# A hybrid decoder layer in fp32 on one core: low weight parts of the first attention on VectorE, and its background steps spread anew

## The chip, the core and the metric

The kernel runs on one core of a Trainium2 chip. The metric is the time of one execution on the device in microseconds (us), from the first to the last instruction and what lies around them. Three runs of the kernel before took 1514.23, 1518.8 and 1519.63 us; the median is 1518.8 us. The engines are named as in the profile: PE is TensorE (matmuls, with PEld its weight loads), DVE is VectorE, ACT is ScalarE, POOL is GpSimd, and SP issues the DMAs.

## What is computed

One layer on 1024 tokens of width 2048: an RMS norm with a shift and a scale that come from a conditioning vector c, one input projection into eight parts, a gated branch (spatial mixing in chunks of 128), an attention branch (window of 128, 16 query heads, 4 key heads, a learned sink), one output projection, a gate, and a last norm with a second shift and scale.

```python
shift, scale, gate = split(silu(c) @ w_ada + b_ada, 3)
h = rms_norm(x, norm_g) * (1 + scale) + shift
u, v, z_a, q, k, v_b, z_b = split(h @ w_in)
y_a = u * (tril(W_s) @ layer_norm(v) + b)
y_b = window_attention_with_sink(rope(q), rope(k), v_b)
x = x + gate * (concat(y_a * silu(z_a), y_b * silu(z_b)) @ w_out)
out = rms_norm(x, final_norm_g) * (1 + scale_f) + shift_f
```

## The kernel before

The tokens are worked in two halves of 512. Every fp32 product is made of three matmuls (`mm3`, L205 to L208): both operands are split into a high part, rounded to the matmul's own format, and a low part, the rest. For the weights this is done as they come in: `chunk` (L127) fetches 128 x 1024 values by DMA, and `split_w` (L138) makes of each 128 x 512 tile a high part with ACT (L148) and a low part, "lo" below, by one subtraction (L149). There are three buffers for each part. The engine of the subtraction is POOL where `on_pool` holds, else DVE.

The input projection is cut into groups of 512 columns (u0, u1, kv, q0, q1, va0, va1, zb0, zb1, za0, za1). `project` (L265) makes one group for one half of the tokens: 16 steps ("kt") of 12 matmuls, a split for each, a DMA for every second. `half(h, kq)` (L766) runs half h: q1, va1, zb0, zb1, u0, u1, za0, za1, then the output projection. Attention is a generator (`attention`, L394, 32 units and 3 steps of tail): from the seventh step of q1 on, `tick` (L242) advances it at 0.58 units per kt, so that its small matmuls stand between those of q1, va1, zb0 and zb1. Its softmax is a chain over PE, DVE and ACT: scores (L335, L336), their least value (DVE L339, L341), exponentials (ACT L343, L344), sums and division (DVE L345 to L348), transposes (PE L355), a split (ACT L359, DVE L360), values (PE L367, L368), and the sum into y (DVE L375, L376). The rotary embedding (`rope`, L287) uses DVE and POOL in turn, also in the background of q1, va1 and zb0. u0 carries the spatial mixing.

Beside that runs the background `bg`: generators whose steps `project` calls after every second kt (`bgn`, L279 and L280). In the first half it holds, in this order, `corr_bg` (8 steps: a row of the shift is loaded into the one tile `misc` by L202, two pieces of the va weights by L736, and four products with sums by DVE L742; at its end a transpose by PE, L195), `gate_bg` (32 steps: one piece of the adaLN weights by L160 and one product with a sum by DVE, L165, a "gate multiply" below) and `stat_bg` (8 steps). A scheduler sets each engine's final order from the program order and priorities; the engines then run their rows strictly in that order.

In the first half alone (`h == 0`) the lo of the weights from q1 to u0 are made by POOL (L788, L821).

```python
lo_pool[0] = h == 0
q1 = project(["q1"], ["mm"], bgn=(0, 1) if h else (1,), after_kt=start)["q1"]
ps = project(["va1"], ["mm"], bgn=(0, 1) if h else (1,))["va1"]
silu_gate(project(["zb0"], ["mm"], bgn=(0, 1) if h else (1, 1, 1, 1, 1, 1, 2, 1))["zb0"], 4, 16)
zb1 = project(["zb1"], ["mm"], bgn=(h,), after_kt=ln_step)["zb1"]
```

Of the kernel before, what the change touches and what calls it, by code (L numbers as in the profile page):

```python
# [31 lines left out]
def R(t):  # L32
    return t.bitcast(F32R)
# [3 lines left out]
def hybrid_layer(ctx: ExitStack, tc: tile.TileContext, A, out):  # L37
# [22 lines left out]
    def four(tag):  # L60
        return banks8[tag]
# [56 lines left out]
    def flat(t):  # L118
        return t.rearrange("p a b -> p (a b)")

    lo_pool = [False]
    ahead = [False]

    def boost():
        return tc.high_priority() if ahead[0] else nullcontext()

    def chunk(src):  # L127
        r = turn_of(raws)
        nw[0] += 1
        with boost():  # L130
            if nw[0] < 3:
                for i in range(2):
                    sp.dma_start(out=r[:, i, :], in_=src[:, i, :])
            else:
                sp.dma_start(out=r, in_=src)
        return r

    def split_w(r, kk, keep=None, on_pool=False):  # L138
        i = nw[1] % 3
        nw[1] += 1  # L140
        with boost():
            if keep is not None:
                act.activation(R(keep[:, :256]), r[:, kk, 256:], AF.Copy)
                dve.tensor_tensor(R(keep[:, 256:512]), r[:, kk, 256:], keep[:, :256], op=ALU.subtract)
                act.activation(R(w_hi[i][:, :256]), r[:, kk, :256], AF.Copy)
                dve.tensor_tensor(R(w_lo[i][:, :256]), r[:, kk, :256], w_hi[i][:, :256], op=ALU.subtract)
                return R(w_hi[i]), R(w_lo[i])
            act.activation(R(w_hi[i]), r[:, kk, :], AF.Copy)  # L148
            (pool if on_pool else dve).tensor_tensor(R(w_lo[i]), r[:, kk, :], w_hi[i], op=ALU.subtract)  # L149
        return R(w_hi[i]), R(w_lo[i])  # L150
# [54 lines left out]
    def mm3(o, lh, ll, rh, rl, first, last):  # L205
        pe.matmul(o, lhsT=lh, rhs=rh, start=first, stop=False)  # L206
        pe.matmul(o, lhsT=lh, rhs=rl, start=False, stop=False)  # L207
        pe.matmul(o, lhsT=ll, rhs=rh, start=False, stop=last)  # L208

    Hh, Hl = [None] * KT, [None] * KT  # L210

    def feature_major(ps, c, W, kt):
        w = slice(c * P, c * P + P)
        mm3(ps, W[0][:, w], W[1][:, w], R(Hh[kt]), R(Hl[kt]), kt == 0, kt == KT - 1)

    def token_major(ps, t, W, kt, w, opens=True, closes=True):
        tk = slice(t * P, t * P + P)
        mm3(ps, R(Hh[kt])[:, tk], R(Hl[kt])[:, tk], W[0][:, w], W[1][:, w], opens and kt == 0, closes and kt == KT - 1)

    def kt_step(g, banks, W, kt):  # L220
        if g == "kv":
            for c in range(2):
                feature_major(banks[c], c, W, kt)
            for t in range(4):
                token_major(banks[2 + t // 2][:, (t % 2) * 256:(t % 2) * 256 + 256], t, W, kt, slice(256, 512),
                            t % 2 == 0, t % 2 == 1)
        elif g in ("va0", "va1"):
            for t in range(4):
                token_major(banks[t], t, W, kt, slice(0, 512))
        else:  # L230
            for c in range(4):
                feature_major(banks[c], c, W, kt)
# [9 lines left out]
    def tick():  # L242
        credit[0] += credit[1]
        while credit[0] >= 1 and side:
            credit[0] -= 1
            try:
                next(side[0])
                settle()
            except StopIteration:
                side.pop(0)  # L250
# [6 lines left out]
    def background(n):  # L257
        while n > 0 and bg:
            try:
                next(bg[0])  # L260
                n -= 1
            except StopIteration:
                bg.popleft()

    def project(gs, tags, per_kt=None, bgn=None, after_kt=None, pool_lo=(), steps=None):  # L265
        banks = {g: four(t) for g, t in zip(gs, tags)}
        raw = {}
        for kt, g in steps or [(kt, g) for kt in range(KT) for g in gs]:
            if g == gs[0] and per_kt is not None:
                per_kt(kt)  # L270
            if (g, kt // 2) not in raw:
                raw[g, kt // 2] = chunk(A["win"][GI[g], kt // 2])
            W = split_w(raw[g, kt // 2], kt % 2, on_pool=lo_pool[0] or (g in pool_lo and kt > 1))
            kt_step(g, banks[g], W, kt)
            if g == gs[-1]:
                if after_kt is not None:
                    after_kt(kt)
                tick()
                if bgn and kt % 2:  # L279
                    background(bgn[kt // 2 % len(bgn)])  # L280
        return banks

    def grab(dst, ps):
        with tc.high_priority():
            act.activation(dst, ps, AF.Copy)
# [14 lines left out]
    def k_stack(parts, j):  # L300
        h1, h2, l1, l2 = parts
        rs = slice(32 * j, 32 * j + 32)
        for k, (a, b) in ((K1[j], (h1, h2)), (K2[j], (l1, l2))):
            for r, s in enumerate((a, b, a, b)):
                sp.dma_start(out=k[32 * r:32 * r + 32, P:], in_=s[rs])
# [72 lines left out]
    def x_pair(kv):  # L378
        return Y[4 + kv][:, 0, :], Y[4 + kv][:, 1, :]
# [6 lines left out]
    def rope_q(kv):  # L386
        parts[kv] = rope(*x_pair(kv), *tpair(kv), *cs)

    def stack(kv, pair):
        Qs[kv, pair] = q_stack(parts[kv], pair)  # L390
# [87 lines left out]
    def settle():  # L478
        while waiting and done[0] >= waiting[0][1]:
            z_mul(waiting.pop(0)[0])  # L480

    def silu_gate(ps, base, need=0):
        for c in range(4):
            with tc.high_priority():
                act.activation(zz[c], ps[c], AF.Silu)  # L485
        waiting.append((base, need))
        settle()
# [197 lines left out]
    for kt in range(KT):  # L685
        g1_kt(kt)
        if kt % 2 == 0:
            raw = chunk(A["win"][GI["va0"], kt // 2])
        W = split_w(raw, kt % 2, on_pool=kt > 1)
# [76 lines left out]
    def half(h, kq):  # L766
        ahead[0] = True
        done[0], credit[0], credit[1] = 0, 0.0, 0.0
        for i, n in enumerate(("cos", "sin")):
            sp.dma_start(out=cs[i], in_=A[n][h])  # L770
        for i in range(2):
            grab(zz[2 + i], kq["kv"][i])

        def q_grab(ps, kvs):
            for i in range(4):
                grab(x_pair(kvs[i // 2])[i % 2], ps[i])

        q_grab(kq["q0"], (0, 1))
        kparts = rope(zz[2], zz[3], zz[0], zz[1], *cs)
        k_stack(kparts, 0)  # L780
        rope_q(0)
        stack(0, 0)
        v_stage(kq["kv"][2:])
        stack(0, 1)
        for j in range(1, 4):
            k_stack(kparts, j)

        lo_pool[0] = h == 0  # L788
        side.append(attention(h))

        def start(kt):
            if kt == 6:
                credit[0], credit[1] = 0.0, 0.58

        q1 = project(["q1"], ["mm"], bgn=(0, 1) if h else (1,), after_kt=start)["q1"]
        q_grab(q1, (2, 3))
        ps = project(["va1"], ["mm"], bgn=(0, 1) if h else (1,))["va1"]
        for t in range(4):
            grab(Y[t][:, 1, :], ps[t])
            if h:  # L800
                sp.dma_start(out=Y[t][:, 0, :], in_=v_d[t])
        silu_gate(project(["zb0"], ["mm"], bgn=(0, 1) if h else (1, 1, 1, 1, 1, 1, 2, 1))["zb0"], 4, 16)
        ln = norm_v(h)

        def ln_step(kt):
            if kt >= 4:
                next(ln, None)

        zb1 = project(["zb1"], ["mm"], bgn=(h,), after_kt=ln_step)["zb1"]
        for _ in ln:  # L810
            pass
        silu_gate(zb1, 6, 32)
        held = [rings.popleft(), rings.popleft()]
        wr = prep_spatial(h, held)
        side.append(spatial(*wr))
        ps = project(["u0"], ["mm"], bgn=(h,))["u0"]
        drain()
        rings.extend(held)
        if h == 0:
            join()  # L820
        lo_pool[0] = False  # L821
        u_gate(ps, 0, S_[:4])
        u_gate(project(["u1"], ["mm"], bgn=(1,))["u1"], 2, S_[4:])
        silu_gate(project(["za0"], ["mm"], bgn=(1,))["za0"], 0)

        def release(kt):
            frr(Hh[kt], Hl[kt])

        ps = project(["za1"], ["mm"], bgn=(1,), after_kt=release)["za1"]
        split_y((4, 5, 6, 7))  # L830
        split_y((0, 1))
        silu_gate(ps, 2)
        split_y((2, 3))
        if h:
            background(1000)
            fr(*[cb[:, 512 * i:512 * i + 512] for i in range(4)])
        out_phase(h)
# [94 lines left out]
```

## Time and profile before

| | before |
|---|---|
| median of three runs | 1518.8 us |
| the profiled execution: its time, its span | 1516.88 us, 1515.1 us |
| busy in the span: PE, DVE, ACT, POOL | 1447.4, 960.8, 629.8, 256.2 us |
| TensorE's granted clock, mean | 0.99 |
| q1 to u0 of the first half: length, DVE busy, POOL busy | 308.3, 200.3, 136.0 us |
| q1 to u0 of the second half: length, DVE busy, POOL busy | 278.7, 216.6, 28.1 us |

Busy time is time in which the engine works on at least one instruction; matmuls are pipelined and their ends are modelled, so a busy PE is not PE at its peak. A stretch here begins with the first matmul of one group and ends with the first matmul of the next. In an engine's row a releaser (<-) is what ended its idle time. Line numbers are those of the kernel before.

### The profile page before, as it was taken

Reading aid. Unit: us, or ns where it says so; the run is one execution under the profiler, and the core shown is the slowest. Engines: PE = TensorE matmul, PEld = TensorE weight load, DVE = VectorE, ACT = ScalarE, POOL = GpSimd, SP = SyncE. Lnnn points to the kernel's source line nnn. Section 1 sums busy time; section 2 is a strip of 40 time slices with the busy share of each in tenths; the row PEclk is TensorE's granted clock in tenths of the full one; section 3 lists DMA queues with packets and bytes.
Section 4 is the critical chain, followed back from the end, with each engine's and each line's share of the span. In section 5 each row is a group of like instructions: output and inputs, shape, how many; then the busy total and the mean of one; then the engine's idle time right before and its main releaser. Section 6 shows DMA issues by size and latency. Waiting matters only on the chain. (4 is left out here: it accounts for less than half of the span.)

```text
span 1515.1 us, 20294 instructions
## 1 busy us (share of the span) xinstructions
PE 1447.4 (96%) x7049; PEld 1208.2 (80%) x7049; DVE 960.8 (63%) x1905; ACT 629.8 (42%) x1397; POOL 256.2 (17%) x184
## 2 busy tenths in 40 slices
PE   7998999888899999999999999999999999999997
PEld 5777877767688888888888978878888878888897
DVE  6879774688763353333466556888796555556456
ACT  3443335454664223432334323666764222332341
POOL 1322164433535100110000101000101001010002
PEclk9999999999999999999999999999999999999999
DMA  9978765556523366733555756544445666665422
GB/s 360 343 294 287 275 190 144 182 172 222 174 70 119 125 198 195 262 120 104 172 159 190 242 184 180 180 126 138 147 154 173 198 211 207 210 229 194 140 84 111
DMA packets 90409, 282.74 MB, mean 187 GB/s; under 512 B 12273, under 2 KB 12865, under 8 KB 90306
## 3 DMA queue, kind: packets, MB, share of 16 engines
q1 hardware_dynamic: 90162, 280.92, 57.0%
q8 instruction: 55, 0.90, 0.2%
q10 hardware_dynamic: 144, 0.52, 0.1%
q14 instruction: 48, 0.39, 0.1%
HBM read 254.10 MB, written 14.72 MB: 177 GB/s over the span
## 5 line engine op out<-in xcount | busy, mean ns | idle before, releaser
L208 PE MATMUL mm<-r,wl 128*128 128x512 f32 x1024 | 401.1, 392 | 9.0 <-DVE wl L149 4.8
L206 PE MATMUL mm<-r,wh 128*128 128x512 f32 x1024 | 402.2, 393 | 5.0 <-ACT wh L148 2.5
L207 PE MATMUL mm<-r,wh 128*128 128x512 f32 x1024 | 400.6, 391 | 0.0
L148 ACT ACTIVATE wh<-wr 128x512 fp32r<-128x512 f32 x324 | 201.7, 627 | 355.7 <-PE mm L207 195.2
L208 PEld LDWEIGHTS mm<-r,wl 128*128 128x128 f32 x1024 | 192.9, 188 | 55.1 <-DVE wl L149 8.7
L149 DVE TENSOR_TENSOR wl<-wr,wh 128x512 fp32r<-128x512 f32 x220 | 154.8, 708 | 127.6 <-ACT wh L148 117.2
L206 PEld LDWEIGHTS mm<-r,wh 128*128 128x128 f32 x1024 | 193.1, 189 | 44.8 <-ACT wh L148 3.4
L207 PEld LDWEIGHTS mm<-r,wh 128*128 128x128 f32 x1024 | 193.2, 189 | 37.4
L149 POOL TENSOR_TENSOR wl<-wr,wh 128x512 fp32r<-128x512 f32 x104 | 151.3, 1459 | 293.8 <-ACT wh L148 271.6
L206 PE MATMUL mm<-wh,r 128*128 128x512 f32 (+1 forms) x448 | 169.1, 381 | 8.0 <-ACT wh L148 8.0
L207 PE MATMUL mm<-wl,r 128*128 128x512 f32 (+1 forms) x448 | 171.3, 382 | 4.9 <-POOL wl L149 4.9
L208 PE MATMUL mm<-wh,r 128*128 128x512 f32 (+1 forms) x448 | 169.9, 380 | 0.0
L207 PE MATMUL att<-wl,r 128*128 128x512 f32 (+1 forms) x448 | 160.7, 359 | 0.0
L206 PE MATMUL att<-wh,r 128*128 128x512 f32 (+1 forms) x448 | 160.5, 358 | 0.0
L208 PE MATMUL att<-wh,r 128*128 128x512 f32 (+1 forms) x448 | 160.4, 359 | 0.0
L149 DVE TENSOR_TENSOR wl<-ring,wh 128x512 fp32r<-128x512 f32 x120 | 88.5, 741 | 89.7 <-ACT wh L148 86.4
L148 ACT ACTIVATE wh<-ring 128x512 fp32r<-128x512 f32 x120 | 75.0, 627 | 150.0 <-PE mm L207 66.6
L476 POOL TENSOR_TENSOR y<-y,t 128x512 f32<-128x512 f32 x32 | 47.6, 1512 | 377.3 <-ACT t L485 367.6
L206 PEld LDWEIGHTS mm<-wh,r 128*128 128x128 f32 x448 | 85.6, 191 | 25.2 <-ACT wh L148 10.0
L207 PEld LDWEIGHTS mm<-wl,r 128*128 128x128 f32 x448 | 86.1, 192 | 22.3 <-POOL wl L149 7.5
L208 PEld LDWEIGHTS mm<-wh,r 128*128 128x128 f32 x448 | 85.8, 192 | 15.1
L206 PEld LDWEIGHTS att<-wh,r 128*128 128x128 f32 x448 | 84.5, 189 | 13.9
(205 smaller groups left out, 1991.8 us busy)
## 6 DMA issues: line engine op xcount, KB each, us to landing
wr<-win SPq DMA_DIRECT2D x127, 512.0 KB, 4.2
ring<-ada SPq DMA_DIRECT2D x94, 512.0 KB, 5.3
wr<-ada SPq DMA_DIRECT2D x51, 512.0 KB, 4.3
wr<-wout SPq DMA_DIRECT2D x38, 512.0 KB, 3.7
ring<-win SPq DMA_DIRECT2D x37, 512.0 KB, 4.2
ring<-wout SPq DMA_DIRECT2D x26, 512.0 KB, 3.7
t<-xT SPq DMA_DIRECT2D x40, 256.0 KB, 5.8
y<-xn SPq DMA_DIRECT2D x20, 512.0 KB, 5.2
```

Of the source, the lines that this page charges most:

```text
L148: act.activation(R(w_hi[i]), r[:, kk, :], AF.Copy)
L149: (pool if on_pool else dve).tensor_tensor(R(w_lo[i]), r[:, kk, :], w_hi[i], op=ALU.subtract)
L206: pe.matmul(o, lhsT=lh, rhs=rh, start=first, stop=False)
L207: pe.matmul(o, lhsT=lh, rhs=rl, start=False, stop=False)
L208: pe.matmul(o, lhsT=ll, rhs=rh, start=False, stop=last)
L476: pool.tensor_tensor(y, y, zz[c], op=ALU.mult)
```

## The change

The subtraction for the low parts goes to DVE for q1, va1, zb0, zb1 and u0 of the first half too (80 of them; the 24 of the first va0 and q0 groups stay on POOL). The background of the first half is called for one step per four kt in va1 and zb0 (4 steps each, where there were 8 and 9), and for one step per two kt in zb1 (8 steps, where there was none). q1 (8 steps) and u0 (none) stay. So 24 steps are called up to u0, where 25 were. Nothing changes in what is computed.

```diff
-    lo_pool = [False]
...
-            W = split_w(raw[g, kt // 2], kt % 2, on_pool=lo_pool[0] or (g in pool_lo and kt > 1))
+            W = split_w(raw[g, kt // 2], kt % 2, on_pool=g in pool_lo and kt > 1)
...
-        lo_pool[0] = h == 0
         side.append(attention(h))
...
-        ps = project(["va1"], ["mm"], bgn=(0, 1) if h else (1,))["va1"]
+        ps = project(["va1"], ["mm"], bgn=(0, 1))["va1"]
...
-        silu_gate(project(["zb0"], ["mm"], bgn=(0, 1) if h else (1, 1, 1, 1, 1, 1, 2, 1))["zb0"], 4, 16)
+        silu_gate(project(["zb0"], ["mm"], bgn=(0, 1))["zb0"], 4, 16)
...
-        zb1 = project(["zb1"], ["mm"], bgn=(h,), after_kt=ln_step)["zb1"]
+        zb1 = project(["zb1"], ["mm"], bgn=(1,), after_kt=ln_step)["zb1"]
...
-        lo_pool[0] = False
```

What the scheduler makes of it stands here at two places (in the changed kernel every line below L121 has a number lower by one, below L788 by two). The first is DVE in va1 of the first half, between the products of the third row of the shift and those of the fourth. Before, the kernel has them back to back:

```order
370 L742 ISA ring_95,corr_86<-ring_95,t_137,corr 128x512
371 L742 ISA corr_86 128x1
372 L742 ISA ring_95,corr_86<-ring_95,t_137,corr 128x512
373 L742 ISA corr_86 128x1
374 L742 ISA ring_96,corr<-ring_96,t_137,corr_86 128x512
375 L742 ISA corr 128x1
```

With the change:

```order
404 L741 ISA ring_95,corr_86<-ring_95,t_137,corr 128x512
405 L741 ISA corr_86 128x1
406 L148 TENSOR_TENSOR wl_102<-wr_93,wh_99 128x512
407 L338 ISA t_126,nm_s_1786<-att_68,mask,nsnk 128x256
408 L338 ISA nm_s_1786 128x1
409 L338 ISA t_126,nm_s_1786<-att_68,mask,nsnk 128x256
410 L338 ISA nm_s_1786 128x1
411 L340 TENSOR_TENSOR e_s_1788<-snk,nm_s_1786 128x2
412 L344 TENSOR_TENSOR d_s_1787<-d_s_1787,e_s_1788 128x2
413 L741 ISA ring_96,corr<-ring_96,t_137,corr_86 128x512
```

A lo (wl) and the front of a softmax (t_126) now stand between the two; `t_137` is `misc`, which both read. All 16 products of the four rows now stand between the fifth and the thirteenth lo of va1, two to a lo. The gate multiplies are hardly moved: the scheduler places 3 in va1, 13 in zb0, none in zb1 and 2 in u0, where the trace of before shows 5, 13, none and 1.

The second place is PE in the eleventh kt of va1, where the sum of all those products (`corr`) is transposed. Before:

```order
1242 L207 MATMUL mm_63<-wl_102,r_140 128x512
1243 L208 MATMUL mm_63<-wh_99,r_141 128x512
1244 L195 MATMUL att_70<-ident,corr 16x128
1245 L206 MATMUL mm_64<-wh_99,r_140 128x512
1246 L207 MATMUL mm_64<-wl_102,r_140 128x512
```

With the change:

```order
1251 L207 MATMUL mm_63<-wh_99,r_141 128x512
1252 L205 MATMUL mm_64<-wh_99,r_140 128x512
1253 L206 MATMUL mm_64<-wl_102,r_140 128x512
1254 L194 MATMUL att_70<-ident,corr 16x128
1255 L207 MATMUL mm_64<-wh_99,r_141 128x512
```

The transpose stands two matmuls later, in the same kt; DVE must by then have made the lo of the next kt as well, since the last product stands behind it in DVE's order.

## Rows read from the trace of the kernel before

**Rows 1.** The page, part 1: busy us (share of the span) and instructions of PE.

```profile
PE 1447.4 (96%) x7049; PEld 1208.2 (80%) x7049; DVE 960.8 (63%) x1905; ACT 629.8 (42%) x1397; POOL 256.2 (17%) x184
```

**Rows 2.** Windows, first half: q1, va1, zb0, zb1, u0; columns in the first line.

```profile
core 0: us, PE busy (x) PEld busy (x) DVE busy (x) ACT busy (x) POOL busy (x), PEclk, DMA share, GB/s
209.60:264.20 54.60, 51.14 (x231) 40.80 (x230) 32.59 (x64) 26.75 (x68) 29.90 (x22) 0.97 0.48 129
264.20:338.20 74.00, 62.65 (x304) 50.59 (x303) 55.31 (x150) 37.44 (x110) 28.82 (x20) 0.93 0.58 174
338.20:402.70 64.50, 57.99 (x293) 48.03 (x291) 54.12 (x142) 36.71 (x108) 23.97 (x17) 0.97 0.68 214
402.70:465.60 62.90, 58.63 (x304) 49.69 (x304) 42.35 (x125) 38.34 (x108) 28.84 (x24) 0.97 0.29 89
465.60:517.90 52.30, 52.30 (x270) 44.63 (x269) 15.90 (x28) 16.42 (x30) 24.45 (x18) 1.00 0.38 122
```

**Rows 3.** Windows, second half: q1, va1, zb0, zb1, u0, in the same columns.

```profile
916.90:967.70 50.80, 48.97 (x233) 40.60 (x233) 37.62 (x81) 24.70 (x59) 6.43 (x5) 1.00 0.61 185
967.70:1028.40 60.70, 58.46 (x314) 49.36 (x313) 53.29 (x140) 39.30 (x109) 6.51 (x4) 1.00 0.42 129
1028.40:1084.60 56.20, 56.20 (x302) 48.03 (x301) 42.61 (x129) 37.62 (x106) 1.32 (x2) 1.00 0.45 134
1084.60:1143.20 58.60, 56.67 (x302) 47.83 (x300) 54.72 (x159) 39.66 (x108) 7.36 (x8) 1.00 0.48 155
1143.20:1195.60 52.40, 52.30 (x266) 44.26 (x267) 28.40 (x44) 16.30 (x30) 6.49 (x4) 1.00 0.57 186
```

**Rows 4.** Waits of PE, first half, q1 to u0 (209.6:517.9): us, times, longest.

```profile
PE att L355 <- DVE r L360: 14.0, 6, 4.5
PE att L195 <- DVE corr L742: 4.3, 1, 4.3
PE mm L208 <- POOL wl L149: 2.7, 2, 2.0
```

**Rows 5.** Waits of PE, second half, q1 to u0 (916.9:1195.6).

```profile
PE att L355 <- DVE r L360: 2.2, 2, 2.1
```

**Rows 6.** Windows of the lo (L149) alone: sum over the second half's five stretches.

```profile
sum 278.70, DVE 58.01 POOL 0.00; mean DVE 11.60 POOL 0.00
```

**Rows 7.** Windows of DVE's L341 alone: va1 and zb0 of the first half.

```profile
264.20:338.20 74.00, 4.12 (x8) 0.93 0.58 174
338.20:402.70 64.50, 3.90 (x11) 0.97 0.68 214
```

**Rows 8.** Windows of DVE's L345 alone: va1 and zb0, then zb0 of the second half.

```profile
264.20:338.20 74.00, 2.49 (x9) 0.93 0.58 174
338.20:402.70 64.50, 3.98 (x10) 0.97 0.68 214
...
1028.40:1084.60 56.20, 1.54 (x10) 1.00 0.45 134
```

**Rows 9.** Windows of L165 (multiply and read-out): first half's zb0, second half's zb1.

```profile
338.20:402.70 64.50, 20.09 (x26) 0.97 0.68 214
...
1084.60:1143.20 58.60, 8.96 (x14) 1.00 0.48 155
```

**Rows 10.** Groups of DVE by form, va1 (264.2:338.2): busy, mean ns, idle before, releaser.

```profile
L742 DVE CUSTOM_DVE_ANT_0 ring<-ring,t,corr 128x512 f32<-128x512 f32 x12 | 9.5, 832 | 9.0 <-DMA t<-rows_d 9.0
...
L742 DVE CUSTOM_DVE_ANT_0 ring<-ring,t 128x512 f32<-128x512 f32 x4 | 2.5, 689 | 3.5 <-DMA t<-rows_d 3.5
```

**Rows 11.** Timeline, DVE, then POOL, near 321 us: start, us, operation.

```profile
321.37 1.24 DVE L345 TENSOR_TENSOR d_s<-d_s,e_s 128x2 f32<-128x2 f32 x1
...
321.16 1.43 POOL L289 TENSOR_TENSOR t<-y,t 128x512 f32<-128x512 f32 x1 [0.30 <-DVE r L360]
```

**Rows 12.** Timeline, DVE, va1: the first product of the fourth row.

```profile
305.79 0.75 DVE L742 CUSTOM_DVE_ANT_0 ring<-ring,t,corr 128x512 f32<-128x512 f32 x1 [5.08 <-DMA t<-rows_d]
```

**Rows 13.** Windows: the last stretch of low clock in zb1.

```profile
417.20:420.60 3.40, 3.40 (x15) 2.97 (x14) 3.37 (x13) 2.55 (x9) 1.30 (x1) 0.50 0.00 0
```

## The prediction, made before the changed kernel ran

> **What bounds the kernel now.** The page comes first: PE is busy for 1447.4 us, 96% of the span [rows 1]. A gain can come only from time in which PE stands or runs slowly, and from a place that the change touches: q1 to u0 of the first half. The windows compare it with the same five projects of the second half, where DVE already makes the lo. There is the same number of matmuls in both, yet the first half takes 54.6, 74.0, 64.5, 62.9 and 52.3 us [rows 2] and the second 50.8, 60.7, 56.2, 58.6 and 52.4 [rows 3]: 308.3 against 278.7, so 29.6 us more, all of it in the first four. Note the granted clock too: 0.93 to 0.97 in these four, 1.00 in the second half.
>
> The waits of PE name what is missing. In the first half it waits 14.0 us for the split of the probabilities (DVE L360), 4.3 us for `corr` and 2.7 us for a lo of POOL [rows 4]; in the second, 2.2 us for L360 [rows 5]. So POOL's lo itself is seldom late; what is late is DVE, in attention's chain. Each long wait costs more than itself: behind the 4.3 us wait for L360 in zb1 the clock stood at 0.50 (1.2 in place of 2.4 GHz) for 3.4 us while PE was busy throughout [rows 13], so about 1.7 us more. The profile shows such stretches only in the first half of these two.
>
> Why is DVE late, with 55.3 of 74.0 us busy in va1 and 54.1 of 64.5 in zb0 [rows 2]? Two reasons show. One is POOL. At 321.37 us a sum of 128x2 values (L345) takes 1.24 us; POOL began a product at 321.16 us that took 1.43 [rows 11]. Ten of these sums take 3.98 us in zb0 of the first half and 1.54 us in zb0 of the second, where POOL is nearly idle [rows 8, 3]. The other is `misc`: DVE stands 12.5 us in va1 (9.0 and 3.5) for the four loads of the row [rows 10], the longest time 5.08 us [rows 12], and everything behind stands with it.
>
> **The change, part by part.** The lo that DVE takes over: per project 11.6 us of DVE's time, the mean of the second half's five stretches [rows 6].
>
> What POOL gives back, per project, by the rows that show it. In zb0: L345 3.98 − 1.54 = 2.4 us [rows 8]; L341, an operation of the same size, 3.90 us for 11, which at 0.154 each would be 1.7, so 2.2 [rows 7]; the gate multiplies, 20.09 us for 13 with their read-outs, where 7 of the second half take 8.96, so 13 would take 16.6 and 3.4 come back [rows 9]. Together 8.0 us. In va1: L345 2.49 − 9 x 0.154 = 1.1 [rows 8], L341 4.12 − 8 x 0.154 = 2.9 [rows 7], L742 12 x (832 − 689 ns) = 1.7 [rows 10]: 5.7 us. The rotary embedding's POOL part stays and is credited with nothing.
>
> The background: by DVE's new order two gate multiplies fewer lie in va1 (3 for 5) and as many in zb0 (13). The steps "given to zb1" don't reach it, since the scheduler places them earlier. Their worth is 2 x 1.28 = 2.6 us of DVE in va1 [rows 9], and none in zb0. Their DMAs move with them on SP; no load stands among PE's waits [rows 4], so I cost those at nothing, covered by the buffers ahead of PE; without that cover each would cost what a stop for `misc` does. One step is called later, in u1, where DVE has little to do: nothing as well, covered there by PE's matmuls.
>
> DVE's load is then 55.3 − 5.7 + 11.6 − 2.6 = 58.6 us in va1, 54.1 − 8.0 + 11.6 = 57.7 in zb0. In q1 and zb1 it is below what the second half bears, even with nothing given back for zb1: 42.4 + 11.6 = 54.0 beside 54.7 in 58.6 us [rows 2, 3].
>
> How close to full can DVE run? The fullest project on record is that zb1 of the second half, 54.7 of 58.6 us, 93% [rows 3]. So:
> - **q1**: as the second half's, 54.6 to 50.8, −3.8.
> - **va1**: 58.6 / 0.93 = 63.0, plus the stops for `misc`. Today they last 12.5 us. With the change a lo and parts of a softmax stand between the products of one row and the next, which covers a part: work of some 2 to 4 us against a turn of about 5.1 [rows 12]. But behind each stop there now waits a lo, too, and PE has three buffers of it. I take half, 6.2, between nothing and 12.5. 69.2 for 74.0: −4.8.
> - **zb0**: 57.7 / 0.93 = 62.0 for 64.5: −2.5.
> - **zb1**: as the second half's, 62.9 to 58.6, −4.3.
> - **u0**: 52.3, PE without a pause in both halves; DVE goes from 15.9 to some 27 us: 0.
>
> The sum is −15.4 us. The profiled execution took 1516.88 us (span 1515.1), 1.9 below the median of the three runs, 1518.8; I count from the former: 1516.9 − 15.4 = **1501.5 us**.
>
> The ends: with DVE full in va1 and zb0 and the stops covered, va1 is held by the second half's 60.7 (−13.3) and zb0 by 57.7 (−6.8): −28.2, so 1488.7. With no stop covered va1 takes 75.5 (+1.5), zb0 −2.5, and if q1 and zb1 give half, −4.0: −5.0, so 1511.9.
>
> A rule speaks against the whole direction. Today POOL carries 16 lo per project, and DVE, the engine that is late, is about to carry them instead. By the Trainium skill, "Perfetto Trace Analysis", section "Optimizing Scalar/DVE Operations", work may be worth moving off a saturated DVE, to GpSimd even; the same passage warns that the two share an SBUF read port, so that moving between them might not help. If the first half of that decides, the sum is that of the third rival below; the trace's 3.98 against 1.54 us [rows 8] bears out the warning.
>
> **The rivals.**
> 1. *As fast as the second half.* DVE's extra load never shows at PE, since lo are made up to three ahead. Then all 29.6 us go: 1487.3. For it: the second half's va1 and zb1 run at 88 and 93% DVE with under 2.5 us of waits for it each. Against it: `corr` with its stops is in the first half alone, and zb0 has 13 gate multiplies where the second half's fullest project has 7.
> 2. *Slower: the stops for `misc` stop the lo.* DVE runs strictly in order, so each of four stops now holds up the next lo, and after that every matmul, not attention's alone. If none is covered and each turn shows whole, 4 x 5.1 = 20.4 us, and each drops the clock, 4 x 1.7 = 6.8, va1 takes 63.0 + 27.2 = 90.2, +16.2; zb0 −2.5, q1 and zb1 half, −4.0: +9.7, so 1526.6. It decides the sign once va1 passes 80.5 (74.0 plus the 6.5 that the others give). For it: PE's transpose of `corr` now needs the products behind the twelfth lo. Against it: half of the four turns already have work between them in the new order, and today the stops sum to 12.5, not 20.4.
> 3. *No difference: nothing comes back from POOL.* If the long 128x2 sums have another cause, va1 has 55.3 + 11.6 − 2.6 = 64.3, / 0.93 + 6.2 = 75.3 (+1.3), zb0 65.7 / 0.93 = 70.6 (+6.1), with q1 and zb1 −8.1: −0.7, so 1516.2. Against it: the same rows are short in the second half.
>
> **How the numbers follow.** A measurement of this kernel can tell about 0.5%, 7.6 us, so faster is below 1509.3. The forecast with its ends has 0.66, of which 0.04 lies above 1509.3; rival 1 has 0.16, rival 2 0.07, rival 3 0.11. Faster: 0.62 + 0.16 = 0.78. Same: 0.04 + 0.11 = 0.15. Slower: 0.07. For the range I keep the forecast's ends and reach down to rival 1, leaving out the last two, 0.18: 1487 to 1512.
>
> **What would show it.** In the profile after: q1 near 51, va1 near 69, zb0 near 62, zb1 near 59, u0 unchanged; POOL's lo down to 24 and DVE's up by 80; the 128x2 sums near 0.155 us; DVE over 85% busy in va1 and zb0, with PE's waits now partly for DVE's lo; 13 gate multiplies still in zb0; fewer stretches of low clock. I am wrong in the term on the stops if va1 ends below 63 or above 76, in the load if zb0 ends below 58 or above 65, in the comparison of halves if q1 or zb1 stay above 53 or 61, and wholly if time moves outside q1 to u0.

## The result, and the profile after

The changed kernel takes 1498.55 us in the median of four runs (1497.92 to 1505.41), the kernel before 1518.74 (1514.23 to 1519.63): a ratio of 0.9892, with a 95% interval of 0.9868 to 0.9916. The medians lie 20.2 us apart; the interval allows 13 to 20 us. The forecast was 1501.5 us, 15.4 less than the profiled execution. The profiled execution of the changed kernel took 1498.45 us, its span is 1496.7.

Where the time went shows in the windows, cut at the same places as before. These are q1, va1, zb0, zb1, u0 and, last, za1 of the first half, with the columns of [rows 2]:

```profile
207.50:259.50 52.00, 50.11 (x231) 41.02 (x230) 36.44 (x81) 28.12 (x70) 6.67 (x5) 0.97 0.52 145
259.50:331.10 71.60, 60.45 (x305) 50.24 (x304) 57.30 (x165) 37.65 (x109) 5.77 (x4) 0.93 0.60 181
331.10:387.40 56.30, 55.47 (x293) 46.81 (x291) 51.39 (x151) 36.29 (x106) 0.01 (x1) 1.00 0.68 219
387.40:445.40 58.00, 57.36 (x304) 48.34 (x305) 47.13 (x145) 39.18 (x110) 9.50 (x9) 1.00 0.32 95
445.40:497.70 52.30, 52.30 (x271) 44.62 (x270) 25.26 (x44) 15.56 (x29) 4.74 (x4) 1.00 0.41 131
584.70:631.80 47.10, 45.11 (x194) 35.64 (x194) 16.66 (x26) 22.00 (x41) 7.18 (x6) 1.00 0.71 235
```

Against [rows 2] q1 is 2.6 us shorter, va1 2.4, zb0 8.2, zb1 4.9, and u0 the same: 18.1 in all. zb0 and zb1 have reached the lengths of the second half [rows 3]. va1 has not: it is 71.6 us, and its clock is 0.93, as before. And za1, at which the prediction didn't look, is longer: before, its window read

```profile
605.00:648.60 43.60, 43.60 (x194) 36.12 (x193) 16.70 (x26) 20.73 (x39) 6.79 (x6) 1.00 0.73 241
```

so 3.5 us of the gain are given back there. The projection of kv and q0, ahead of q1, is 1.8 us shorter (96.8 to 95.0). The span is 18.4 us shorter in all, so some 2 us more went in small pieces elsewhere, most of them in the second half.

The waits of PE from q1 to u0, in the columns of [rows 4]:

```profile
PE att L194 <- DVE corr L741: 9.3, 1, 9.3
PE mm L205 <- ACT y L284: 1.8, 1, 1.8
PE mm L206 <- DVE wl L148: 1.5, 1, 1.5
PE att L354 <- DVE r L359: 1.0, 2, 0.6
```

The 14.0 us for attention's split are 1.0 now. What is left is mainly one wait, 9.3 us for `corr`, where 4.3 stood before; in a window around it the granted clock is 0.54 in the mean:

```profile
300.90:312.00 11.10, 6.00 (x22) 5.23 (x23) 9.73 (x24) 4.82 (x13) 2.85 (x2) 0.54 0.67 194
```

DVE's groups by form in va1 (columns of [rows 10]) show the lo at 687 ns each and the stops for the row of the shift at 8.5 us, where 12.5 were:

```profile
L148 DVE TENSOR_TENSOR wl<-wr,wh 128x512 fp32r<-128x512 f32 x16 | 11.0, 687 | 1.8 <-ACT wh L147 1.8
L741 DVE CUSTOM_DVE_ANT_0 ring<-ring,t,corr 128x512 f32<-128x512 f32 x12 | 9.2, 770 | 8.5 <-DMA t<-rows_d 8.5
```

And in the same view of q1 to zb1 the 128x2 sums, 439 ns in the mean before, are at 154 (before, then after):

```profile
L345 DVE TENSOR_TENSOR d_s<-d_s,e_s 128x2 f32<-128x2 f32 x32 | 14.0, 439 | 12.5 <-ACT e_s L344 12.5
...
L344 DVE TENSOR_TENSOR d_s<-d_s,e_s 128x2 f32<-128x2 f32 x32 | 4.9, 154 | 5.1 <-ACT e_s L343 5.1
```

The mean before hides two kinds of sum. By the view of that line alone, the middle one of the 32 takes 161 ns and the longest 1280 (least, median, most):

```profile
L345 DVE TENSOR_TENSOR d_s<-d_s,e_s x32: 135/161/1280, 242.2 to 461.0; 128x2 f32<-128x2 f32 x32
```

Set beside POOL's timeline they fall apart cleanly: nine of the 32 begin while a subtraction of POOL or a product of its rotary embedding is under way, take 1.16 us in the mean and end about 0.02 us after POOL's instruction; the other 23 take 0.16. An operation with one input (the reciprocal, L346: 0.16 us) or with one input in PSUM, the memory of matmul results (L360: 0.69 us), takes the same time in both cases.

The gate multiplies (L164 with its read-outs) do not lie where they were counted. Their windows in va1 and zb0, in the columns of [rows 9]:

```profile
259.50:331.10 71.60, 5.78 (x9) 0.93 0.60 181
331.10:387.40 56.30, 14.82 (x24) 1.00 0.68 219
```

Five begin in va1, as before, the last of them 0.6 us before its end; eleven begin in zb0, none in zb1 and two in u0. The scheduler's order had been read as 3, 13, none and 2; the windows are cut by PE's matmuls, and the two counts differ.

### The profile page after: what moved, and what is told of

Its sections match the earlier page's. It is cut to its first block, busy times and chain, and to the rows that moved or that the text cites. A ratio compares the mean times of both kernels' runs of the same rounds, so it can differ in the third digit from the quotient of the medians.

```text
span 1496.7 us, 20247 instructions
## 1 busy us (share of the span) xinstructions
PE 1440.8 (96%) x7049; PEld 1205.4 (81%) x7049; DVE 979.8 (65%) x1985; ACT 630.7 (42%) x1397; POOL 144.9 (10%) x104
## 5 line engine op out<-in xcount | busy, mean ns | idle before, releaser
L147 ACT ACTIVATE wh<-wr 128x512 fp32r<-128x512 f32 x318 | 197.6, 626 | 320.2 <-PE mm L206 180.9
L148 DVE TENSOR_TENSOR wl<-wr,wh 128x512 fp32r<-128x512 f32 x294 | 211.3, 722 | 167.1 <-ACT wh L147 151.4
L147 ACT ACTIVATE wh<-ring 128x512 fp32r<-128x512 f32 x126 | 79.1, 629 | 172.2 <-PE mm L206 87.4
L475 POOL TENSOR_TENSOR y<-y,t 128x512 f32<-128x512 f32 x32 | 47.5, 1510 | 524.0 <-ACT t L484 507.5
L206 PEld LDWEIGHTS att<-wl,r 128*128 128x128 f32 x448 | 84.5, 189 | 14.0
```

Of the source, the lines that this page charges most:

```text
L475: pool.tensor_tensor(y, y, zz[c], op=ALU.mult)
```

## The experiments

Three questions were open: which half of the change gave the gain, and through what; what holds va1; and why za1 grew. Ratios are to the kernel before.

**Which half: the lo alone, the table alone.** The first kernel has the lo on DVE and the old table; the second has the new table and the lo on POOL. Both diffs are against the kernel before.

```diff
-            W = split_w(raw[g, kt // 2], kt % 2, on_pool=lo_pool[0] or (g in pool_lo and kt > 1))
+            W = split_w(raw[g, kt // 2], kt % 2, on_pool=g in pool_lo and kt > 1)
```

> The low parts go to VectorE as in the change; the background table stays that of the kernel before (8 steps in va1, 9 in zb0, none in zb1). Theory: the gain is the lo's engine, through GpSimd's hold on VectorE's sums, and the table is worth nothing up to u0. Then q1 52, va1 72 (within 3), zb0 57, zb1 58.5 us, and za1 stays at 43.7 since the 25th step is back: 1495 to 1499. Rival (the table is what relieves VectorE in va1 and zb0): va1 above 75, zb0 above 62, 1506 or more.

Measured: 1495.35 us (1493.18 to 1496.61), ratio 0.9849 [0.9824, 0.9875]. q1, va1, zb0 and zb1 take 50.5, 70.5, 57.2 and 57.0 us. The lo alone does it all, and the table of the change is of no use; this kernel lies 3.2 us below the change in the median, though the two intervals overlap a little. One figure missed: za1 takes 45.7 us and not 43.7, with 25 steps called up to u0 again.

```diff
-        ps = project(["va1"], ["mm"], bgn=(0, 1) if h else (1,))["va1"]
+        ps = project(["va1"], ["mm"], bgn=(0, 1))["va1"]
...
-        silu_gate(project(["zb0"], ["mm"], bgn=(0, 1) if h else (1, 1, 1, 1, 1, 1, 2, 1))["zb0"], 4, 16)
+        silu_gate(project(["zb0"], ["mm"], bgn=(0, 1))["zb0"], 4, 16)
...
-        zb1 = project(["zb1"], ["mm"], bgn=(h,), after_kt=ln_step)["zb1"]
+        zb1 = project(["zb1"], ["mm"], bgn=(1,), after_kt=ln_step)["zb1"]
```

> The new background table alone; the low parts of the first attention stay on GpSimd. Theory: no gain up to u0 (within 3 us of 308), the 128x2 sums still at 0.3 us and more in the mean, and za1 about 3 us longer as in the changed kernel: 1517 to 1522. Rival (the table relieves VectorE): va1 and zb0 together at least 8 us shorter, 1509 or less.

Measured: 1517.81 us in ten runs, ratio 0.9994 [0.9978, 1.0011]: nothing. q1 to zb1 are 54.5, 72.4, 62.3 and 62.6 us, so 4.2 shorter together, which the expectation put within 3, and za1 takes 47.0, 3.4 longer. The 128x2 sums stay at 439 ns. So in the profile the table does two small things that cancel, and za1 grows by it without the lo.

**Through what: POOL does the subtraction a second time.** The changed kernel, with each of the 80 subtractions done by POOL as well, into a tile that nobody reads (`also` holds from q1 to u0 of the first half). The instructions of DVE and of PE are those of the change, in the same order from q1 to zb1 in both traces.

```diff
             (pool if on_pool else dve).tensor_tensor(R(w_lo[i]), r[:, kk, :], w_hi[i], op=ALU.subtract)
+            if also[0]:
+                pool.tensor_tensor(spare, r[:, kk, :], w_hi[i], op=ALU.subtract)
```

> The changed kernel, with GpSimd doing each of the 80 subtractions a second time into a tile that nobody reads. VectorE's own list is that of the change. Theory (GpSimd's reads hold VectorE's sums up): the 128x2 sums of the first attention go from 0.155 back to 0.3 us or more in the mean, VectorE's busy time in va1 and zb0 rises by 4 to 8 us each, and the time by 6 to 20 us: 1505 to 1519. Rival (the old lo was late because GpSimd is slow, 1.4 against 0.7 us, and the sums were long for another reason): sums at 0.155, 1497 to 1501.

Measured: 1546.08 us (1543.64 to 1554.71), ratio 1.0198 [1.0162, 1.0234]: 47.5 us above the change, slower than before, and far outside the 1505 to 1519 that were expected. DVE's groups from q1 to zb1 say why, the lo of the change first:

```profile
L148 DVE TENSOR_TENSOR wl<-wr,wh 128x512 fp32r<-128x512 f32 x65 | 47.7, 735 | 22.4 <-ACT wh L147 19.9 <-PE att L335 1.4 <-PE att L354 0.9
...
L150 DVE TENSOR_TENSOR wl<-wr,wh 128x512 fp32r<-128x512 f32 x65 | 75.2, 1163 | 15.3 <-ACT wh L149 15.3
L348 DVE TENSOR_TENSOR d_s<-d_s,e_s 128x2 f32<-128x2 f32 x32 | 18.0, 563 | 4.9 <-ACT e_s L347 4.9
```

The sums are back at 563 ns, and the lo themselves go from 735 to 1163 ns in the mean. Again there are two kinds: 33 of the 65 lo begin while an instruction of POOL is under way and take 1.62 us in the mean, the other 32 take 0.69. With them PE's wait for attention's split is back, 1.0 us in the change:

```profile
PE att L358 <- DVE r L363: 19.7, 9, 4.4
```

With q1 to zb1 at 59.8, 82.7, 69.4 and 68.8 us, DVE is busy for 72.0 and 65.5 in va1 and zb0, 14 us more in each where 4 to 8 were expected. That POOL at work beside DVE lengthens DVE's operations, and that the wait in attention's chain follows, is shown, with the order of both engines unchanged. The size was misjudged: the doubled subtraction meets the lo themselves, which POOL's subtractions before could not, as DVE made none there. (The tiles wh and wr are also held longer in this kernel; how much of the 47.5 us that makes wasn't separated.) By the Trainium skill, "SBUF — State Buffer", section "Who interferes with whom", a DVE instruction with two SBUF inputs contends with a GpSimd instruction that reads SBUF, since its second input comes through a read interface that the two engines share; the page calls the shared ports an exclusive lock, and says that the order of issue decides who is blocked. The trace agrees: the sums take 154 ns alone and 563 in the mean beside POOL, the long ones begin second and end with POOL's instruction, and operations with one SBUF input are not lengthened.

**va1: is it the transpose's place?** The changed kernel, with `corr`'s transpose two gate columns later, in the fifth step of zb0.

```diff
-        to_row(4, corr)
...
         for kt in range(KT):
+            if kt == 2:
+                to_row(4, corr)
             yield from mod_col("gate", kt, gate_c[:, kt:kt + 1])
```

> The changed kernel with the transpose of corr, and the store of its row, called two gate columns later, so that it stands in the fifth step of zb0 on TensorE in place of the eleventh of va1. Theory: the 9.3 us that TensorE stands for corr, and the clock that it loses behind it, are the transpose's place and not VectorE's load: no wait of over 3 us is left in va1, which falls from 71.6 to 61 to 65 us, zb0 56 to 58, 1488 to 1492. Rival (VectorE's backlog with its stops for the row bounds va1 by itself): the low parts are late in the transpose's stead, va1 stays at 68 or more, 1495 or more.

Measured: 1500.63 us (1495.64 to 1502.76), ratio 0.9884 [0.9855, 0.9913]: as the change. The wait moved to attention's split, at almost the same size in all though in four parts, and va1 stayed at 70.0 us. PE's waits in va1 of this kernel:

```profile
PE att L354 <- DVE r L359: 9.1, 4, 4.6
```

The theory fell, and its rival holds in the main: DVE is late in va1, and PE meets that at another instruction that needs it. That instruction is attention's split, though, and not the lo that the rival named.

**va1: the stops, taken away.** A second tile for the row, so that the next row's load doesn't wait for the products with this one.

```diff
+    misc2 = st([P, 512], "misc2")
...
-            load_row(3, pc, misc)
+            row = (misc, misc2)[pc % 2]
+            load_row(3, pc, row)
...
-                    dve.tensor_tensor_reduce(ti, ti, misc, scale=1.0, scalar=prev,
+                    dve.tensor_tensor_reduce(ti, ti, row, scale=1.0, scalar=prev,
```

> The changed kernel with a second tile for the row of the shift, so that a row's load no longer waits for the products with the row before. Theory (the stops for the row, 8.6 us of VectorE in va1, are what keeps va1 long, whatever matmul they show at): the stops fall below 3 us, TensorE's wait for corr or L359 falls from 9 to under 4 us, va1 from 71.6 to 61 to 66 us, 1488 to 1494. Rival (the products themselves and the lo fill VectorE): stops gone, va1 still 68 or more, 1495 or more.

Measured: 1489.43 us (1485.96 to 1490.03), ratio 0.9808 [0.9782, 0.9833], so 9.1 us below the change. The windows of va1 and zb0, and DVE's products by form in va1:

```profile
258.10:320.70 62.60, 58.04 (x304) 48.02 (x303) 57.62 (x168) 38.88 (x111) 5.68 (x4) 1.00 0.67 212
320.70:375.80 55.10, 55.10 (x293) 46.94 (x292) 49.48 (x148) 36.55 (x107) 0.92 (x1) 1.00 0.73 223
```

```profile
L743 DVE CUSTOM_DVE_ANT_0 ring<-ring,misc,corr 128x512 f32<-128x512 f32 x8 | 5.9, 746 | 0.7 <-DMA ring<-wvaT 0.6
L743 DVE CUSTOM_DVE_ANT_0 ring<-ring,t,corr 128x512 f32<-128x512 f32 x4 | 2.9, 737 | 0.0
L743 DVE CUSTOM_DVE_ANT_0 ring<-ring,t 128x512 f32<-128x512 f32 x4 | 2.7, 686 | 0.7 <-DMA t<-rows_d 0.7
```

DVE does the same work, 57.6 us busy against 57.3, but in 62.6 us and not 71.6: 92% full, with 0.7 us left of the stops, and PE's wait for `corr` is down from 9.3 us to 0.3. The clock stays at 1.00, so the 9.0 us by which va1 is shorter include the low stretch behind the wait.

```profile
PE att L195 <- DVE corr L743: 0.3, 1, 0.3
```

**va1: its floor.** The changed kernel without the 16 products (this leaves out the sum `corr`; the loads stay).

```diff
-                    dve.tensor_tensor_reduce(ti, ti, misc, scale=1.0, scalar=prev,
-                                             op0=ALU.mult, op1=ALU.add, accum_out=acc_)
```

> The changed kernel without the 16 products with the row (VectorE, 12 us with their read-outs) and so without their stops; it leaves out that sum, and the loads stay. It gives the floor of va1 with the lo on VectorE. Theory: va1 57 to 61 us as in the second half, at the full clock, zb0 and zb1 as in the change, 1484 to 1489. Rival (va1 is long for the weights' lo and attention's chain alone): va1 65 or more.

Measured in one run: 1493.02 us, va1 63.1, zb0 55.9, zb1 57.1. Both va1 and the time lie above what was expected; za1, at 48.8 us, is 1.7 longer than in the change. The window of va1:

```profile
258.30:321.40 63.10, 58.24 (x304) 48.74 (x303) 50.06 (x138) 38.15 (x111) 6.36 (x4) 0.99 0.67 201
```

DVE is busy for 7.2 us less than in the change and 7.6 less than with two tiles, yet va1 is no shorter than with the products and two tiles. So, as far as one run shows, the products themselves cost nothing, and the stops were all of it.

**The second tile, with the late transpose, and with the old table.** Two combinations, of edits shown above.

> The second tile for the row, and the transpose of corr two gate columns later. Theory: with the stops gone the transpose's place matters little; va1 59 to 63 us, within 3 us of the kernel with the second tile alone. Rival (place and stops each cost by themselves): at least 4 us below that kernel.

Measured: 1492.28 us (1489.9 to 1494.36), ratio 0.9833 [0.981, 0.9855], va1 61.8: with the stops gone the place of the transpose gives nothing.

> The lo on VectorE and the second tile for the row, with the background table of the kernel before. Theory: the table is worth at most 3 us, and that in za1, which is 1.4 to 2 us shorter with the old table's 25 steps: 1485 to 1492, within 3 us of the kernel with the second tile and the new table. Rival (the new table keeps VectorE free once the stops are gone): at least 4 us above that kernel.

Measured: 1488.6 us (1484.38 to 1491.32), ratio 0.9806 [0.9781, 0.9832], as with the new table. The parts differ by more than was expected: va1 and zb0, at 64.0 and 56.4 us, are 1.4 and 1.3 longer than with the new table, and za1 is 5.4 shorter. It is the old one again:

```profile
572.80:616.40 43.60, 43.60 (x194) 36.12 (x193) 16.68 (x26) 20.89 (x39) 6.83 (x6) 1.00 0.74 240
```

**za1.** The new table calls 24 steps up to u0, one fewer than the old; the background's last steps, which fetch x and let ACT square it, end one step later, in za1. ACT's waits in za1 of the kernel before, then of the changed one (who <- for whom: us, times, longest):

```profile
ACT wr L174 <- DMA wr<-xn: 9.2, 3, 3.4
...
ACT ring L174 <- DMA ring<-xn: 5.5, 2, 3.5
```

```profile
ACT wr L173 <- DMA wr<-xn: 11.9, 4, 3.3
ACT ring L173 <- DMA ring<-xn: 7.7, 2, 4.7
```

Five loads for 14.7 us against six for 19.6; the weights' high parts (L147) stand behind them on ACT, and PE waits for these, 1.9 us in the changed kernel's za1. With the second tile, and a step added to zb0 so that 25 are called again:

```diff
-        silu_gate(project(["zb0"], ["mm"], bgn=(0, 1))["zb0"], 4, 16)
+        silu_gate(project(["zb0"], ["mm"], bgn=(0, 1) if h else (0, 1, 0, 1, 0, 1, 1, 1))["zb0"], 4, 16)
```

> The second tile for the row and the new table with one step more in zb0, so that 25 are called up to u0 again. With 24, ScalarE has eight squares of x (L174) from the first kt of za1 on, the last two in neighbouring kts near its end; with 25 it has one fewer there, as with the old table. Theory (za1's 3 to 5 us more are ScalarE standing for the loads of these squares, behind which the weights' high parts wait): za1 43.6 to 45 us, 1484 to 1488. Rival (za1 is longer because of where the lo, on VectorE, leave the ring's tiles): za1 at 47 or more.

Measured: 1484.8 us (1482.47 to 1487.78), ratio 0.9781 [0.9748, 0.9814]. za1 falls from 49.0 to 45.3 us, short of the 43.6 of the old table, with five waits for loads:

```profile
ACT wr L174 <- DMA wr<-xn: 8.5, 3, 3.2
ACT ring L174 <- DMA ring<-xn: 8.0, 2, 5.7
```

The theory holds in direction, and the step is worth 3.7 us here. Over all kernels, one profile of each, za1 takes 43.6 to 45.7 us where 25 steps are called up to u0 and 46.9 to 50.6 where 24 are; between pairs that differ by the table alone it grows by 1.4 us (the lo alone to the change), 3.4 (before to the table alone) and 5.4 (with two tiles). So the step is the main cause, and its price varies; why it does, and what makes ACT wait up to 5.7 us for a single load, stays open. This is the fastest kernel of the study, 33 us below the kernel before and 13.8 below the change, though its lead over the same kernel with the old table (1488.6) is within their spread. More steps earlier were tried too:

```diff
-        ps = project(["u0"], ["mm"], bgn=(h,))["u0"]
+        ps = project(["u0"], ["mm"], bgn=(1,) if h else (0, 1))["u0"]
```

> The second tile for the row and the new table with u0 of the first half given one step per four kt, 28 steps up to u0, so that the squares start in za0 and end in the seventh kt of za1. Theory: za1 at 43.6 us, u0 at 52.3, since VectorE is under half busy there, 1483 to 1487. Rival (u0 holds two of the three ring tiles, so that loads and spatial mixing collide): u0 or za0 longer by 2 us or more, nothing gained.

Measured: 1491.74 us (1486.73 to 1495.46), ratio 0.9827 [0.9794, 0.9859]. za1 is 43.7 us, as the theory had it, and za0 45.5, 2.0 longer than in the change, with ACT waiting 14.4 us for loads of x there: the waits moved with the loads, and the time is no lower.

## Why the prediction was right, point by point

- **The bound and the place** were read rightly: attention's chain on DVE, in the four projects where the two halves differ. The forecast of −15.4 became −18.1 us over q1 to u0 in the profile. That the time of the profiled execution came within some 3 us of the forecast is in part luck: zb0 gave 5.7 us more than forecast, q1 and va1 gave 3.6 less, and outside q1 to u0, where the prediction looked for no change, +3.5 us in za1 met −1.8 in kv and q0 and about −2 elsewhere.
- **What POOL gives back** held as a mechanism. L345 gave back all of the 2.4 us in zb0 (1.54 us for ten after). The kernel in which POOL subtracts too shows the cause by bringing it back, with the wait for attention's split.
- **q1**, −3.8 forecast, −2.6 measured, and 50.4 to 50.5 us in most of the other kernels with the lo on DVE, where the clock didn't fall: the term's size is right, and this execution had one stretch of low clock more.
- **zb0** is the term that was mis-sized: −2.5 forecast, −8.2 measured, and by the prediction's own sign, zb0 below 58, the load was wrong. The divisor was fair (91% full, where 93% was put); the load was 57.7 us forecast, 51.4 measured. The gate multiplies are 1.8 us of it, by place and not by size: 20.09 us fell to 14.82 and not to 16.6, because eleven begin in zb0 and the end of one more lies there, where 13 were counted. Operations of attention and the rotary embedding that now lie outside this window (L293, L295, a step of L339) are some 2 us. Another part is how durations were added. In a full queue DVE begins the next instruction before the last one ends, as its timeline in zb0 of the changed kernel shows (start, us):

```profile
367.90 0.69 DVE L148 TENSOR_TENSOR wl<-wr,wh 128x512 fp32r<-128x512 f32 x1
368.50 0.15 DVE L340 TENSOR_TENSOR e_s<-snk,nm_s 128x2 f32<-128x2 f32 x1
368.57 1.27 DVE L164 CUSTOM_DVE_ANT_0 ring<-ring,cb,pc_s 128x1024 f32<-128x1024 f32 x1
```

  A lo of 0.69 us takes 0.60 of the engine's time here, a sum of 0.15 takes 0.07. So 11.6 us of lo added to busy time were too many: 16 lo at 0.60 are 9.6, an estimate from these rows, 2 us less.
- **va1** came out at 71.6 us for 69.2. Its load came near, 58.6 forecast and 57.3 measured, by errors that cancel. The two gate multiplies did not leave va1: five begin there before and after, and 0.65 us went where 2.6 were forecast. L341 gave back 1.8 us of 2.9, since it was priced at 154 ns where the second half's va1 shows 267, and L742 0.7 of 1.7. On the other side the division of the softmax (L348, from 602 to 418 ns) and the rotary embedding on DVE (L291, L293), credited with nothing, gave back about 3 us. The guess that half of the stops are covered was generous: 8.5 of 12.5 us remained, and PE met them in one wait, at the transpose, with 10 us of low clock around it. The second tile for the row prices them: 9.0 us of va1.
- **zb1** −4.9 for −4.3, **u0** 0 for 0.
- **The background** "at nothing" failed: up to zb1 the table gave 4.2 us without the lo and nothing with it, and the one step called later was not covered by PE's matmuls, in za1 and not in u1. za1 grew by 3.5 us, through ACT, which the prediction had looked at nowhere.
- **The rivals.** *As fast as the second half* came true for zb0 and zb1 and failed for va1, for the reason named against it. *Slower* did not decide, though the stops cost 9 us of va1; they showed at the transpose of `corr`, which it had named, and hardly at the lo, for which PE waits 1.5 us. *Nothing comes back from POOL* fell with the sums at 154 ns, and with the kernel that has POOL subtract too.

## What to carry to other kernels

Before moving work between two engines, look for short instructions that are long beside the other engine: if they shrink where that engine is idle, the move can give back more than its own time takes. Look at the stops of an engine that runs in order, and not only at its load: here va1 went from 71.6 to 62.6 us with the same busy time of DVE once a row's load had a second tile, and moving the instruction that showed the wait did nothing. A table of background steps has an end as well as a beginning: ask where its last steps land when one is taken out.

## What was not expected of the hardware

What POOL at work costs a DVE operation with two inputs in SBUF is what is left of POOL's instruction, whatever the operation's own size. A 128x2 sum of 0.16 us that begins while POOL works on a 128x512 tile took 1.16 us in the mean before the change, and a lo of 0.69 us took 1.62 in the kernel where POOL subtracts too; the others kept their 0.16 and 0.69. So the shortest instructions suffer most. And DVE can be 91 to 92% busy over a whole project (51.4 of 56.3 us in zb0 of the change, 57.6 of 62.6 in va1 with two row tiles) while PE waits for it by nothing and by 2.3 us, with about 1 us in each in which DVE stands for a load.
